# Keys' transposes in another bank, two held steps and a first copy that frees others, in a two-layer hybrid decoder trunk

## The chip, the cores and the metric

The kernel runs on one core of a Trainium2 chip. The metric is device microseconds from start to end of one execution, as the median of several. A core has five engines that run their own instruction rows and wait for each other by semaphores: TensorE (PE; its weight loads are listed as PEld), VectorE (DVE), ScalarE (ACT), GpSimd (POOL) and SyncE (SP), which here only issues transfers. Operands lie in on-chip memory; TensorE writes its results into eight banks of an accumulation memory of 128 x 512 numbers each, from where VectorE and ScalarE read them.

## What is computed

Two layers of a decoder over 256 tokens of width 1024, in 32-bit floats. The core of the reference:

```
for l in range(DEPTH):
    xn = rms_norm(h, norm_mix[l])
    proj = xn @ w_in[l]
    (hq, hf, hi, hg, nq, kc, vc, ksl, vsl, ksw, vsw, ngate) = jnp.split(proj, IN_SPLIT_POINTS, axis=-1)
    o_hg = hgrn2_mixer(hq, hf, hi, hg, lb[l], hg_gnorm[l])
    o_nsa = nsa_mixer(nq, kc, vc, ksl, vsl, ksw, vsw, ngate, ...)
    mix = jnp.concatenate([o_hg, o_nsa], axis=-1)
    h = h + mix @ w_out[l]
    xn = rms_norm(h, norm_ffn[l])
    gu = xn @ w_ffn_in[l]
    h = h + (jax.nn.silu(gu[..., :D_FF]) * gu[..., D_FF:]) @ w_ffn_out[l]
```

The hgrn2 mixer is a gated linear recurrence of 4 heads of 128 (q, forget gate f, input i, output gate g); the nsa mixer has 8 query heads of 64 in two groups and three branches (compressed, selected and sliding-window attention), each with a softmax, weighted by gates. With 256 tokens the selected and the window branch both see all causal keys.

## The kernel before

**Products in three parts.** Each weight matrix comes in units of 128 x 1024 numbers (`unit`, `load_to`). A unit is split into a high part, a rounded copy by ScalarE (`whi`, line 144), and a low part, a subtraction by VectorE (`wlo`, line 145); activations are split the same way. `mm3` (line 330) issues three matmuls per product: high by high, high by low, low by high. All of them are appended to the list `products`, and other steps are tied to a place in it: `after(a, [products[n]])` puts instruction a behind the n-th product in the scheduler's graph, without a wait of its own. Raw loads lie in 4 buffers, split units in 6; `weights(i)` splits up to 5 units ahead of the one in use, so a split may start once the unit six places earlier has been read for the last time.

**The order.** The code names priorities and ties, and a scheduler puts each engine's instructions in one fixed row. Each engine runs its row in that order.

**One layer.** `norm_T` normalises x, turns it on TensorE (`pxn`, line 357), and splits it (`x2`; high part line 362 on ScalarE, low part line 363 on VectorE). The projections follow in the order B (compressed keys and values, selected keys), C (window keys and values, gates), A (queries), first gates, second gates, hi, hg, the output projection `py`, and the feed-forward part (`pgu`, `pz`). In the second layer the first pxn transposes are tied behind product `end + HOLD[0]`, which lies in the last sums of the layer before (`pz`), and the products of C stand partly among those of B.

**Attention, beside the products.** `phid` and `phT`, `pkc` are the compression network; `pkT` its turned key; `pkk` (line 580) the turned selected and window keys, copied to `kA` (ScalarE, line 586) and `kB` (VectorE, line 587); `pqT` the turned queries, copied to `qA`. `scores(t, g)` makes the scores `pS` (for t = 0 a mask matmul first, line 638), the negated maximum `nm`, and the exponentials (`exps`, line 608, ScalarE) with their sums; line 664 and 666 scale them by `cf` on VectorE and ScalarE. `compressed()` is the small branch (`pcs`, `scT`, `pcr`, `pc`, `pcT`). `outputs(t)` turns the probabilities (`pPT`, line 678), copies them to `PT` (ScalarE for g = 0, VectorE for g = 1, line 682) and sums `pO` (line 690).

**Recurrence, beside the products.** From the gates (`FH`, `KH`, `QH`) `pd` and seven levels `pl` (line 806) build the matrix `AT`; VectorE multiplies the decays between levels, and ScalarE copies the levels 6 and 7 into `AT` (line 834). `vh` is the copy of the hi projection (line 759, ScalarE), `sgt` that of hg.

**Banks.** Eight banks under four tags: "a" 2, "b" 2, "c" 3, "e" 1. A tile of a tag waits until the tile that used its bank before has been read. hi and hg use "a" (a bank for each of the two halves of the tokens, so hg's first half takes the bank of hi's first half); pkT, pkk, pqT, pS, pPT, pcs, pcr, pcT use "c"; C, pd, pl use "b".

Of the kernel before, what the change touches and what calls it, by code (L numbers as in the profile page):

```python
# [14 lines left out]
AF = mybir.ActivationFunctionType  # L15
# [3 lines left out]
D, T, NT, NL = 1024, 256, 2, 2  # L19
# [21 lines left out]
AHEAD = 5  # L41
SPLIT_PRIO = 400
LEV_PRIO, BLOCK_PRIO, PACE = 250, 3000, (6, 14)
HOLD, HOLD_C, HOLD_T = (18, 18, 16, 36), 1, 28


def shape_constants():
# [43 lines left out]
def trunk(ctx: ExitStack, tc: tile.TileContext, x, w_in, w_out, lbl, gnorm, q_gain, k_gain,  # L91
          pe_k, w1_k, w2_k, pe_v, w1_v, w2_v, w_ffi, w_ffo, norm_mix, norm_ffn, consts, out):
    nc = tc.nc
    V, S, PE, DMA = nc.vector, nc.scalar, nc.tensor, nc.sync
# [10 lines left out]
    def bank(name, tag):  # L105
        return ps.tile([128, 512], F32, name=name, tag=tag, bufs=BANKS[tag])
# [2 lines left out]
    units = []  # L109

    def unit(src, a, b):
        units.append([src, a, b, None, None, None, None])
        return len(units) - 1

    state = {"loaded": 0, "split": 0}
# [12 lines left out]
    def after(ins, others):  # L128
        for o in others:
            tc.add_manual_dep(ins.ins, o.ins.name,  # L130
                              mybir.DependencyInfo(mybir.DependencyClass.NoSync, mybir.DependencyReason.DATA),
                              reason="fewer table loads")

    def split_to(n):
        while state["split"] < min(n, len(units)):
            load_to(state["split"] + 1)
            u = units[state["split"]]
            a, b = u[1], u[2]
            hi = wsp.tile([128, 1024], F32R, name="whi")
            lo = wsp.tile([128, 1024], F32R, name="wlo")  # L140
            u[4] = hi[:, : a * b].rearrange("p (a b) -> p a b", b=b)
            u[5] = lo[:, : a * b].rearrange("p (a b) -> p a b", b=b)
            with tc.high_priority(offset=SPLIT_PRIO):
                after(S.activation(u[4], u[3], AF.Copy), hi_behind.pop(0) if hi_behind else ())  # L144
                u[6] = V.tensor_sub(u[5], u[3], u[4].bitcast(F32))  # L145
                if lo_behind:
                    after(u[6], lo_behind.pop(0))
                    lo_held.append(u[6])
            state["split"] += 1
# [222 lines left out]
    for l in range(NL):  # L372
# [39 lines left out]
        def proj_tok(name, n=512, tag="a"):  # L412

            for t in range(NT):
                p = bank("pt", tag)
                ts = slice(128 * t, 128 * t + 128)
                for q in range(4):
                    w = weights(U[name, q]) if t == 0 else units[U[name, q]][4:6]
                    for k in range(2):
                        kk = 2 * q + k  # L420
                        mm3(p[:, :n], (X[0][:, kk, ts], X[1][:, kk, ts]), (w[0][:, k], w[1][:, k]),
                            kk == 0, kk == KC - 1)
                yield t, p
# [24 lines left out]
        for t, p in proj_tok("B"):  # L448
            if l and t == 0:
                norm_T(1, gain0, *X[:2], "c", hold=begin + HOLD[1])  # L450
            S.activation(kvc[:, t], p[:, 0:256].rearrange("p (a d) -> p a d", d=64)[:, :, None, :]
                         .to_broadcast([128, 4, 2, 64]), AF.Copy)
            square_k(p[:, 256:384], 0, t)
            S.activation(vtok[:, 0, t], p[:, 384:512], AF.Copy)
            rope_k(p[:, 256:384].rearrange("p (g d) -> p g d", d=64), 0, t)
# [24 lines left out]

        gate = wk.tile([128, NT, 24], F32, name="gate")
        for t, p in proj_tok("C", 280, "b"):
            S.activation(gate[:, t], p[:, 256:280], AF.Sigmoid)
            square_k(p[:, 0:128], 1, t)
            S.activation(vtok[:, 1, t], p[:, 128:256], AF.Copy)
            rope_k(p[:, 0:128].rearrange("p (g d) -> p g d", d=64), 1, t)
# [87 lines left out]

        k8 = kraw.rearrange("p t b (g d) -> p (t b g) d", d=64)
        V.tensor_mul(k8, k8, rs[:, 16:24, None].to_broadcast([128, 8, 64]))
        p = bank("pkk", "c").rearrange("p (b t s) -> p b t s", b=2, t=NT)
        for b in range(2):
            for t in range(NT):
                PE.transpose(p[:, b, t], kraw[:, t, b], ident)  # L580
# [36 lines left out]
        for t in range(NT):  # L617
            nm[t] = sm.tile([128, 2, 4, 2], F32, name="nm")
            rsum[t] = sm.tile([128, 2, 4, 2], F32, name="rsum")
            cf[t] = sm.tile([128, 2, 4, 2], F32, name="cf")  # L620

        def exps(t, p, g, hg):
            for b in range(2):
                exp(P[t, g][:, hg, b], p[:, b], bias=nm[t][:, g, hg, b:b + 1],
                    accum_out=rsum[t][:, g, hg, b:b + 1])

        def scores(t, g):
            if t == 0:
                if g == 0:
                    P0 = wk.tile([128, 2, 4, 2, 128], F32, name="P0", tag="big", bufs=3)  # L630
                    for gg in range(2):
                        P[0, gg] = P0[:, gg]
            else:
                P[1, g] = wk.tile([128, 4, 2, 256], F32, name="P1", tag="big", bufs=3)
            if t == 0:
                for hh in range(2):
                    p = bank("pS", "c").rearrange("p (h b s) -> p h b s", h=2, b=2)
                    PE.matmul(p.rearrange("p h b s -> p (h b) s"), idb, idb4, start=True, stop=False,
                              skip_group_check=True)
                    for i in range(2):  # L640
                        PE.matmul(p[:, i], qA[t][:, g, 2 * hh + i], kA[:, g, :, 0:128], start=False,
                                  stop=False, skip_group_check=True)
                        PE.matmul(p[:, i], qA[t][:, g, 2 * hh + i], kB[:, g, :, 0:128], start=False,
                                  stop=(i == 1), skip_group_check=True)
                    V.tensor_reduce(nm[t][:, g, 2 * hh:2 * hh + 2].rearrange("p h b -> p (h b)"),
                                    p.rearrange("p h b s -> p (h b) s"), axis=AX.X, op=OP.max, negate=True)
                    for i in range(2):
                        exps(t, p[:, i], g, 2 * hh + i)
            else:
                for hg in range(4):  # L650
                    p = bank("pS", "c").rearrange("p (b s) -> p b s", b=2)
                    PE.matmul(p, qA[t][:, g, hg], kA[:, g], start=True, stop=False, skip_group_check=True)
                    PE.matmul(p, qA[t][:, g, hg], kB[:, g], start=False, stop=False, skip_group_check=True)
                    PE.matmul(p[:, :, 128:256], idb, idb4[:, 0:2], start=False, stop=True, skip_group_check=True)
                    V.tensor_reduce(nm[t][:, g, hg], p, axis=AX.X, op=OP.max, negate=True)  # L655
                    exps(t, p, g, hg)
            c = cf[t][:, g].rearrange("p h b -> p b h")
            V.reciprocal(cf[t][:, g], rsum[t][:, g])
            V.tensor_mul(c, c, gv[:, t, 1:3, :, g])
            for hg in range(4):  # L660
                for b in range(2):
                    x, sc = P[t, g][:, hg, b], cf[t][:, g, hg, b:b + 1]
                    if b == 0:
                        V.tensor_scalar(x, x, sc, None, op0=OP.mult)
                    else:
                        S.activation(x, x, AF.Copy, scale=sc)

        def outputs(t):
            po = bank("pO", "e")
            steps = [(b, sb) for b in range(2) for sb in range(t + 1)]  # L670

            def turned(b, sb):

                pts = []
                for g in range(2):
                    p = bank("pPT", "c")
                    for hg in range(4):
                        last = PE.transpose(p[:, 128 * hg:128 * hg + 128],  # L678
                                            P[t, g][:, hg, b, 128 * sb:128 * sb + 128], ident)
                    pt = turn[:, len(turns) % 4]  # L680
                    turns.append(pt)
                    pts.append((pt, V.tensor_copy(pt, p) if g else S.activation(pt, p, AF.Copy)))
                turned.last = [last]
                return pts

# [72 lines left out]
        for t, p in proj_tok("hi"):  # L758
            S.activation(vh[:, t], p, AF.Copy)  # L759
        after(kT, [products[begin + 7]])  # L760
        sgt = wk.tile([128, NT, 512], F32, name="sgt", tag="vs", bufs=2)
        for t, p in proj_tok("hg"):
            V.tensor_copy(sgt[:, t], p)
# [2 lines left out]
        with tc.high_priority(offset=LEV_PRIO):  # L766
# [18 lines left out]
            for lev in range(1, 8):  # L785
# [45 lines left out]
                for n in range(64 // half):  # L831
                    for i in range(2):
                        r0, s0 = 64 * n + half * i, 2 * half * n
                        S.activation(AT[s0:s0 + half, :, i::2, s0 + half:s0 + 2 * half],
                                     pl[r0:r0 + half, :4 * half].rearrange("p (t h a) -> p t h a", t=NT, a=half), AF.Copy)
            p = bank("p8", "b").rearrange("p (h s) -> p h s", s=128)
            for hd in range(4):
                PE.matmul(p[:, hd], KH[:, hd, 0:128], QH[:, hd, 128:256], start=True, stop=True)
# [217 lines left out]
```

## Time and profile before

| | |
|---|---|
| median of 3 runs | 675.47 us (675.41 to 675.97) |
| profiled execution, its own time | 677.52 us |
| its span, first to last instruction | 675.7 us |
| TensorE busy | 658.1 us, 97% of the span |
| VectorE busy | 458.4 us, 68% |
| ScalarE busy | 380.0 us, 56% |
| GpSimd busy | 30.8 us, 5% |
| granted TensorE clock | 1.000 of full speed |

The profile gives for each engine its instructions with their starts and durations, and for an idle stretch the instruction that ended it. Consecutive instructions of one kind are one row, with their count; the ends of matmuls are modelled and neighbours overlap, so the distance from one start to the next is what a step takes of TensorE's time. A row of several matmuls that is longer than their pitch has a wait inside. Idle time on ScalarE or VectorE costs nothing by itself; what they delay on TensorE does.

### The profile page before, as it was taken

To read this page: it belongs to the slowest core of one execution; us is meant where nothing else is said; L and a number is where in the kernel's file an instruction comes from. 1 tells how busy PE (TensorE), PEld (TensorE's weight loads), DVE (VectorE), ACT (ScalarE), POOL (GpSimd) and SP (SyncE) were. 2 spreads that over 40 slices of the span, in tenths; PEclk is the share of its full clock that TensorE was granted. 3 is DMA by queue.
4 is the path that set the end of the run, shared out by engine and by line. 5 is a ranking of instruction groups with operands and counts; after the bars stand their busy time and mean duration, and the time that the engine had idled before them with its cause. 6 is when DMAs were issued, how large, how long until landed. Compare 5 with 4: busy or idle time off the path is not lost.

```text
span 675.7 us, 11741 instructions
## 1 busy us (share of the span) xinstructions
PE 658.1 (97%) x4607; PEld 551.3 (82%) x4607; DVE 458.4 (68%) x767; ACT 380.0 (56%) x670; POOL 30.8 (5%) x67
## 2 busy tenths in 40 slices
PE   5999999999999999999999999999999999999997
PEld 3879876689888888888878897766898888888886
DVE  4878799767665555555578958987676555555552
ACT  5536786836555555555456558685555555555540
POOL 2700001001000000000010000000000000000000
PEclk9999999999999999999999999999999999999999
DMA  7898633254666656656678742432466666666631
GB/s 243 249 346 260 183 72 119 63 184 131 216 186 189 190 191 195 194 193 192 179 239 289 232 125 65 128 95 63 124 215 191 187 186 187 188 190 188 188 120 63
DMA packets 86575, 118.90 MB, mean 176 GB/s; under 512 B 5036, under 2 KB 69366, under 8 KB 86519
## 3 DMA queue, kind: packets, MB, share of 16 engines
q1 hardware_dynamic: 86518, 118.15, 56.9%
q8 instruction: 36, 0.59, 0.4%
q14 instruction: 21, 0.16, 0.1%
HBM read 117.08 MB, written 1.05 MB: 175 GB/s over the span
## 4 chain that ended last, share of the span: by engine, by line
PE 84%; ACT 5%; DVE 4%; DMA 3%; POOL 3%; issue 2%; SPq 0%; DVEq 0%; ACTq 0%; POOLq 0%
PE pgu L940 21%; PE pz L330 17%; PE pgu L944 11%; PE pt L330 10%; PE py L330 6%; PE pq L330 3%; PE pf L330 3%; PE pO L690 2%; DMA wraw<-in_w_in_dram 2%; PE pgt L330 2%; PE pPT L678 1%; ACT whi L144 1%; DVE wlo L145 1%; PE pl L806 1%; ACT P L608 1%
## 5 line engine op out<-in xcount | busy, mean ns | idle before, releaser
L144 ACT ACTIVATE whi<-wraw 128x1024 fp32r<-128x1024 f32 (+1 forms) x204 | 212.7, 1044 | 176.1 <-PE pgu L940 59.1
L145 DVE TENSOR_TENSOR wlo<-wraw,whi 128x1024 fp32r<-128x1024 f32 (+1 forms) x204 | 242.1, 1206 | 59.3 <-ACT whi L144 58.5
L940 PE MATMUL pgu<-x,whi 128*128 128x512 f32 x640 | 152.7, 390 | 0.0
L940 PEld LDWEIGHTS pgu<-x,whi 128*128 128x128 f32 x640 | 118.6, 188 | 23.6
L330 PE MATMUL pz<-whi,ahl 128*128 128x512 f32 x352 | 112.3, 391 | 0.0
L330 PE MATMUL pt<-whi,x 128*128 128x512 f32 (+1 forms) x320 | 97.0, 381 | 0.0
L944 PEld LDWEIGHTS pgu<-x,wlo 128*128 128x128 f32 x640 | 82.1, 191 | 3.1
L944 PE MATMUL pgu<-x,wlo 128*128 128x256 f32 x640 | 83.0, 283 | 0.0
L330 PEld LDWEIGHTS pz<-whi,ahl 128*128 128x128 f32 x352 | 66.0, 188 | 13.9 <-DVE ahl L958 0.5
L330 PE MATMUL pz<-wlo,ahl 128*128 128x512 f32 x176 | 68.8, 391 | 0.0
L330 PEld LDWEIGHTS pt<-whi,x 128*128 128x128 f32 x320 | 57.4, 190 | 9.8 <-ACT vh L759 0.9
L330 PE MATMUL pt<-wlo,x 128*128 128x512 f32 (+1 forms) x160 | 61.2, 382 | 0.7 <-DVE wlo L145 0.7
L955 DVE TENSOR_TENSOR su<-su,pgu 128x256 f32<-128x256 f32 x40 | 16.7, 418 | 50.5 <-ACT su L954 50.5
L949 DVE TENSOR_TENSOR sl<-sl,pgu 128x256 f32<-128x256 f32 x40 | 16.7, 417 | 50.5 <-ACT sl L948 50.5
L330 PE MATMUL py<-whi,x 128*128 128x512 f32 x128 | 42.5, 400 | 0.0
L330 PEld LDWEIGHTS pz<-wlo,ahl 128*128 128x128 f32 x176 | 33.1, 188 | 6.0
L330 PEld LDWEIGHTS pt<-wlo,x 128*128 128x128 f32 x160 | 30.4, 190 | 5.6 <-DVE wlo L145 1.1
L608 ACT ACTIVATE P<-pS,nm 128x128 f32<-128x128 f32 (+1 forms) x64 | 26.2, 429 | 7.1 <-DVE nm L655 6.2
L330 PEld LDWEIGHTS py<-whi,x 128*128 128x128 f32 x128 | 24.1, 188 | 5.3 <-DVE x L707 0.4
L330 PE MATMUL py<-wlo,x 128*128 128x512 f32 x64 | 25.1, 393 | 0.0
L330 PE MATMUL pf<-x,whi 128*128 128x256 f32 x128 | 24.1, 286 | 0.2 <-ACT whi L144 0.2
L330 PE MATMUL pgt<-whi,x 128*128 128x256 f32 x128 | 23.6, 284 | 0.0
(218 smaller groups left out, 808.8 us busy)
## 6 DMA issues: line engine op xcount, KB each, us to landing
wraw<-in_w_ffn_in_dram SPq DMA_DIRECT2D x88, 512.0 KB, 4.5
wraw<-in_w_in_dram SPq DMA_DIRECT2D x48, 512.0 KB, 5.2
wraw<-in_w_ffn_out_dram SPq DMA_DIRECT2D x44, 512.0 KB, 4.0
w<-in_cmp_w_k_dram SPq DMA_DIRECT2D x8, 512.0 KB, 5.0
w<-in_cmp_w_v_dram SPq DMA_DIRECT2D x8, 512.0 KB, 7.0
wraw<-in_w_out_dram SPq DMA_DIRECT2D x16, 256.0 KB, 4.2
wraw<-in_w_out_dram SPq DMA_DIRECT2D x8, 512.0 KB, 4.7
wraw<-in_w_in_dram SPq DMA_DIRECT2D x8, 280.0 KB, 5.6
```

Of the source, the lines that this page charges most:

```text
L144: after(S.activation(u[4], u[3], AF.Copy), hi_behind.pop(0) if hi_behind else ())
L145: u[6] = V.tensor_sub(u[5], u[3], u[4].bitcast(F32))
L330: products.append(PE.matmul(o, a[u], b[v], start=start and i == 0, stop=stop and i == 2, skip_group_check=skip))
L608: e = S.activation(o, i, f, **kw)
L678: last = PE.transpose(p[:, 128 * hg:128 * hg + 128], P[t, g][:, hg, b, 128 * sb:128 * sb + 128], ident)
L690: m = PE.matmul(po[64 * g:64 * g + 64], vtok[:, b, sb, 64 * g:64 * g + 64], pts[g][0], start=(b == 0 and sb == 0), stop=False, skip_group_ ...
L806: m = PE.matmul(o, a, b, start=True, stop=True)
L940: products.append(PE.matmul(pp[b], w[hh][0][:, k, s], X[2][:, 4 * hh + k].rearrange("p c t -> p (c t)"), start=(hh == 0 and k == 0), stop= ...
L944: products.append(PE.matmul(pp[b][:, T:], w[hh][1][:, k, s], X[0][:, 4 * hh + k], start=False, stop=(hh == 1 and k == 3), skip_group_check ...
L949: V.tensor_add(sl[:, b], sl[:, b], pp[b][:, :T])
L955: V.tensor_add(su[:, b], su[:, b], pp[b][:, :T])
```

## The change

Five edits:

- `pkk` takes a bank of tag "b" instead of "c", and is therefore no longer in a row with pkT and pqT for their banks.
- `HOLD_S = 12`: the first mask matmul of the scores is tied behind the 13th product of hi.
- `HOLD[0]` goes from 18 to 21: the second layer's first pxn transposes are tied three products later.
- In the second layer the high part of the second unit of A is tied behind the copy `kvc` of the second half of the tokens (`kept`); entry 7 of a unit now keeps its high part's instruction.
- The copies of levels 6 and 7 into `AT` are tied behind the first copy `PT` of `outputs(0)` (`freed`).

```diff
-HOLD, HOLD_C, HOLD_T = (18, 18, 16, 36), 1, 28
+HOLD, HOLD_C, HOLD_T, HOLD_S = (21, 18, 16, 36), 1, 28, 12
...
-                after(S.activation(u[4], u[3], AF.Copy), hi_behind.pop(0) if hi_behind else ())
+                u[7] = S.activation(u[4], u[3], AF.Copy)
+                after(u[7], hi_behind.pop(0) if hi_behind else ())
...
-            S.activation(kvc[:, t], p[:, 0:256].rearrange("p (a d) -> p a d", d=64)[:, :, None, :]
+            kept = S.activation(kvc[:, t], p[:, 0:256].rearrange("p (a d) -> p a d", d=64)[:, :, None, :]
...
         for t, p in proj_tok("C", 280, "b"):
+            if l and t == 0:
+                after(units[U["A", 1]][7], [kept])
...
-        p = bank("pkk", "c").rearrange("p (b t s) -> p b t s", b=2, t=NT)
+        p = bank("pkk", "b").rearrange("p (b t s) -> p b t s", b=2, t=NT)
...
-                    PE.matmul(p.rearrange("p h b s -> p (h b) s"), idb, idb4, start=True, stop=False,
-                              skip_group_check=True)
+                    masks.append(PE.matmul(p.rearrange("p h b s -> p (h b) s"), idb, idb4, start=True, stop=False,
+                                           skip_group_check=True))
...
                     pts.append((pt, V.tensor_copy(pt, p) if g else S.activation(pt, p, AF.Copy)))
+                    if not freed:
+                        freed.append(pts[0][1])
...
         after(kT, [products[begin + 7]])
+        after(masks[0], [products[begin + HOLD_S]])
...
-                        S.activation(AT[s0:s0 + half, :, i::2, s0 + half:s0 + 2 * half],
-                                     pl[r0:r0 + half, :4 * half].rearrange("p (t h a) -> p t h a", t=NT, a=half), AF.Copy)
+                        m = S.activation(AT[s0:s0 + half, :, i::2, s0 + half:s0 + 2 * half],
+                                         pl[r0:r0 + half, :4 * half].rearrange("p (t h a) -> p t h a", t=NT, a=half), AF.Copy)
+                        after(m, freed)
```

No instruction is added or taken away; the rows of the engines change their order, and the numbers of lines behind the changes rise by 1 to 11.

**ScalarE, first layer, from the last exponentials of the first half of the queries to the copies of hi.** pt_1228 and pt_1282 are the two halves of hi, whi_1310 and whi_1322 the first and the second unit of the output projection that is split here, pc the compressed branch's scores. Before:

```order
L608 ACTIVATE P0_947,rsum_942<-pS_991,nm_941 128x128 x2
L719 ACTIVATE scT_1029<-pcs_1012 128x256
L144 ACTIVATE whi_1310<-wraw_1233 128x1024
L759 ACTIVATE vh_1227<-pt_1228 128x512
L144 ACTIVATE whi_1322<-wraw_1246 128x1024
L759 ACTIVATE vh_1227<-pt_1282 128x512
L666 ACTIVATE P0_947<-P0_947,cf_943 128x128 x4
L608 ACTIVATE pc_1034<-pc_1034 128x256
```

After:

```order
L144 ACTIVATE whi_1310<-wraw_1233 128x1024
L671 ACTIVATE P0_947<-P0_947,cf_943 128x128 x2
L144 ACTIVATE whi_1322<-wraw_1246 128x1024
L671 ACTIVATE P0_947<-P0_947,cf_943 128x128
L611 ACTIVATE pc_1034<-pc_1034 128x256
L768 ACTIVATE vh_1227<-pt_1228 128x512
L768 ACTIVATE vh_1227<-pt_1282 128x512
```

Both vh copies moved from around whi_1322 to behind it, behind a scaling and behind the exponential of pc.

**TensorE, first layer, at the keys' transposes and the first scores.** pf_811 are the second gates' first products, pd the recurrence's first block. Before:

```order
L567 MATMUL pkT_770<-cst_81,kcb_760 128x32
L580 MATMUL pkk_777<-cst_81,kraw_223 128x128 x4
L594 MATMUL pqT_790<-cst_81,qn_467 128x128 x4
L594 MATMUL pqT_801<-cst_81,qn_467 128x128 x4
L775 MATMUL pd_1386<-Q_221,K_220 32x32 x32
```

After, in two pieces, the keys' transposes and then the queries' and the first scores:

```order
L532 MATMUL phT_737<-cst_81,hid_735 128x64 x2
L583 MATMUL pkk_777<-cst_81,kraw_223 128x128 x4
L331 MATMUL pf_811<-x2_130,whi_575 128x256 x2
...
L570 MATMUL pkT_770<-cst_81,kcb_760 128x32
L597 MATMUL pqT_790<-cst_81,qn_467 128x128 x4
L597 MATMUL pqT_801<-cst_81,qn_467 128x128 x4
L331 MATMUL pt_1228<-whi_842,x2_130 128x512 x2
L785 MATMUL pd_1386<-Q_221,K_220 32x32 x32
```

pkk moved from behind pkT, in the products of hi, to ahead of the second gates.

**VectorE at the start of the second layer.** wlo_3492 and wlo_3504 are the low parts of the third and the fourth unit of B, h the residual, x2_3545 the low part of the turned x. Before:

```order
L145 TENSOR_TENSOR wlo_3492<-wraw_3419,whi_3491 128x1024
L363 TENSOR_TENSOR x2_3545<-pxn_3554,x2_3545 128x4x128
L1022 TENSOR_TENSOR h_76<-pz_2072,h_76 128x512
L363 TENSOR_TENSOR x2_3545<-pxn_3561,x2_3545 128x4x128
L145 TENSOR_TENSOR wlo_3504<-wraw_3425,whi_3503 128x1024
```

After:

```order
L146 TENSOR_TENSOR wlo_3492<-wraw_3419,whi_3491 128x1024
L146 TENSOR_TENSOR wlo_3504<-wraw_3425,whi_3503 128x1024
L1033 TENSOR_TENSOR h_76<-pz_2072,h_76 128x512
L364 TENSOR_TENSOR x2_3545<-pxn_3554,x2_3545 128x4x128
L364 TENSOR_TENSOR x2_3545<-pxn_3561,x2_3545 128x4x128
```

The fourth unit's low part and the addition to h moved ahead of both low parts of x; on ScalarE, in the same way, whi_3503 moved ahead of both high parts of x.

## Rows read from the trace of the kernel before

**Rows 1.** The page's part 1: busy us (share of the span) and instructions, TensorE.

```profile
PE   658.1 (97%) x4607; PEld 551.3 (82%) x4607; DVE 458.4 (68%) x767; ACT 380.0 (56%) x670; POOL 30.8 (5%) x67
```

**Rows 2.** TensorE's waits: instruction, releaser, us in total, times, longest.

```profile
PE pS L638 <- DVE kB L587: 1.0, 2, 0.5
...
PE pkc L541 <- DVE hk L537: 0.8, 1, 0.8
```

**Rows 3.** TensorE's timeline at the first scores: start, us, instruction, count, idle before.

```profile
82.22 0.62 PE L330 MATMUL pt<-whi,x 128*128 128x512 f32 x2
82.67 0.39 PE L330 MATMUL pt<-wlo,x 128*128 128x512 f32 x1
83.57 0.39 PE L638 MATMUL pS<-cab,idb 128*128 128x512 bf16 x1 [0.51 <-DVE kB L587]
```

**Rows 4.** ScalarE's timeline around the copies of hi, first layer.

```profile
96.75 0.58 ACT L759 ACTIVATE vh<-pt 128x512 f32<-128x512 f32 x1
97.39 1.06 ACT L144 ACTIVATE whi<-wraw 128x1024 fp32r<-128x1024 f32 x1
98.36 0.58 ACT L759 ACTIVATE vh<-pt 128x512 f32<-128x512 f32 x1
98.84 1.27 ACT L666 ACTIVATE P<-P,cf 128x128 f32<-128x128 f32 x4
100.86 0.42 ACT L608 ACTIVATE pc<-pc 128x256 f32<-128x256 f32 x1 [0.75 <-DVE pc L732]
```

**Rows 5.** TensorE's timeline from hi to hg, first and second layer.

```profile
96.96 0.91 PE L330 MATMUL pt<-whi,x 128*128 128x512 f32 x2
...
425.47 0.91 PE L330 MATMUL pt<-whi,x 128*128 128x512 f32 x2
```

**Rows 6.** TensorE's timeline in the outputs, first layer.

```profile
112.51 0.66 PE L678 MATMUL pPT<-cst,P 128*128 128x128 f32 x4 [0.31 <-ACT PT L682]
113.10 1.40 PE L690 MATMUL pO<-PT,vtok 128*64 128x512 f32 x4
114.43 0.50 PE L652 MATMUL pS<-kA,qA 128*128 128x512 f32 x1
...
116.75 1.08 PE L690 MATMUL pO<-PT,vtok 128*64 128x512 f32 x4
117.76 1.16 PE L702 MATMUL pO<-pcT_sb,vblk 128*128 128x128 f32 x8
...
127.11 1.61 PE L678 MATMUL pPT<-cst,P 128*128 128x128 f32 x12
...
133.25 1.94 PE L690 MATMUL pO<-PT,vtok 128*64 128x512 f32 x8
```

**Rows 7.** TensorE's timeline at the second layer's start.

```profile
343.75 0.63 PE L357 MATMUL pxn<-cst,xn 128*128 128x128 f32 x4 [0.51 <-DVE xn L345]
...
346.28 0.62 PE L330 MATMUL pt<-whi,x 128*128 128x512 f32 x2
```

**Rows 8.** ScalarE's and VectorE's timelines there.

```profile
343.85 0.18 ACT L339 ACTIVATION_READ_ACCUMULATOR xn<-h 128x1 f32 x1
...
346.33 0.68 ACT L144 ACTIVATE whi<-wraw 128x560 fp32r<-128x560 f32 x1
...
344.18 1.22 DVE L145 TENSOR_TENSOR wlo<-wraw,whi 128x1024 fp32r<-128x1024 f32 x1
...
346.01 0.69 DVE L1022 TENSOR_TENSOR h<-pz,h 128x512 f32<-128x512 f32 x1
```

**Rows 9.** TensorE's timeline at the compression's transposes, second layer.

```profile
359.88 0.87 PE L465 MATMUL pa<-cst,kvc 128*128 128x128 f32 x6 [0.30 <-ACT kvc L451]
```

**Rows 10.** TensorE's timeline at the kernel's start.

```profile
11.12 1.97 PE L357 MATMUL pxn<-cst,xn 128*128 128x128 f32 x8 [4.90 <-DVE xn L345]
...
13.94 1.05 PE L330 MATMUL pt<-whi,x 128*128 128x512 f32 x2
14.79 0.45 PE L330 MATMUL pt<-wlo,x 128*128 128x512 f32 x1
```

More of the change, by code (lines that the diff above doesn't have):

```diff
@@ L111, in unit @@
     def unit(src, a, b):
-        units.append([src, a, b, None, None, None, None])
+        units.append([src, a, b] + [None] * 5)
         return len(units) - 1
@@ L620, in trunk @@
             cf[t] = sm.tile([128, 2, 4, 2], F32, name="cf")
+        masks = []
         def exps(t, p, g, hg):
@@ L666, in scores @@
                         S.activation(x, x, AF.Copy, scale=sc)
+        freed = []
         def outputs(t):
```

## Prediction

> **What bounds the kernel now.** I read the busy shares first, then what TensorE waits for, then the timeline of the places the diff touches. TensorE is busy 658.1 us of a span of 675.7 [rows 1], so the end moves only by what is added to or taken from TensorE's own row: a wait, or an interruption of its row of products. The profiled execution took 677.52 us against a median of 675.47; differences are summed on the former and set on the latter. The list of waits names few in the two attention stages: the scores for kB 1.0 us in two layers, pkc 0.8 [rows 2]. It names no wait where a row of two products simply took longer, and one such row matters below.
>
> **Keys' transposes earlier, first mask held.** In the first layer the last group of products before the first scores starts at 82.67, its scores at 83.57: 0.90 us where a product takes 0.23 (two in the 0.45 from 82.22), of which 0.51 is idle on kB [rows 3]; the 0.16 that is left is what an interruption of the row costs. The wait of pS comes twice, once a layer [rows 2]. In the changed order pkk and its copies run during the second gates, and products stand between pqT and the scores, so kB is long there. I take 0.6 a layer as gained, between 0 (the scores then wait for qA, which is copied in the same few us) and 0.67. The pkc wait (0.8, on hk) stays: pkk's four transposes stand ahead of it, but nothing that makes hk is earlier; a gain of at most 0.5 is left to the range.
>
> **ScalarE around vh: the term that decides.** TensorE's first product of hg writes the bank that hi's first token left, so it waits for the first vh copy. Before, that copy stands ahead of the split of the second of wo's weights (whi_1322): vh starts 96.75, the split 97.39, the second vh 98.36 [rows 4]. After, ScalarE's row is: split, one scaling of P, the exponential of pc, and only then vh. That split writes the memory of the last weights of hi (six buffers in a ring), so it may not start before the 48th, last product of hi has read them; and the 49th may not start before vh. TensorE therefore stands still for the whole chain, whatever else goes well. Before, the row of two from 96.96 took 0.91 us and one product takes 0.39 [rows 3], so the 49th began at 97.48 [rows 5]: 0.52 after the 48th, 0.29 more than the pitch of 0.23. After, from the start of the 48th: 0.43 until the split starts (97.39 less 96.96), 0.97 the split (98.36 less 97.39), 0.32 a scaling (1.27 for four), 0.33 the exponential (0.42 less the 0.09 by which neighbours overlap), 0.58 vh, and 0.15 until TensorE starts (97.48 less 96.75 and 0.58) [rows 4, 5]. The sum is 2.78, a stop of 2.55, so **+2.26 us** a layer. The second layer has the same row of two at 425.47, 0.91 [rows 5], and the changed order is the same there. Bounds: +1.9 if the split is let go 0.1 sooner and the neighbours overlap more, +2.6 if the exponential comes late. The row shows ScalarE taking instructions strictly one behind another. The Trainium skill's page PSUM — Partial Sum Buffer, section Engine vs sequencer instructions, says that too, "ScalarE/VectorE/GpSimdE queues are strict FIFO"; if ScalarE could take vh past the waiting split, this term would be nothing and the sum 675.1, but row and page both speak against that.
>
> **Level 6 and 7 copies held behind the first PT copy.** This turns the whole tail of the attention: the pPT of outputs(0) stand in one row, outputs(1) comes earlier, the levels later. Counts are the same. Before, waits lie in four kinds of places: pPT for PT (112.51, 0.31 idle), pO after it (113.10 to 114.43 is 1.33, where the same four take 1.01 from 116.75 to 117.76) [rows 6], and likewise two rows of pO and pPT of outputs(1); I read them together as an estimate at 1.8 us, from 0.43 and 0.24 around 112.51, 0.32 behind it, and 0.83 in seven rows between the twelve transposes at 127.11 and the eight pO at 133.25, the first and the last of them [rows 6] (1.53 for the twelve where eight take 0.85, and so on). After, pO of outputs(0) waits for VectorE's copy of PT, which stands behind the level's decay (about 1.0), and that of outputs(1) behind the next level's (about 0.85): about the same 1.85. Two interruptions fewer at 0.16 are -0.32, and the last transposes wait a little more (+0.1). I take **-0.15** a layer, between -2.0 (all waits gone) and +0.6. A layer then gives 2.26 - 0.6 - 0.15 = **+1.5**, two layers +3.0. SyncE's issue of w1's fourth part now stands ahead of the last wo load and two ffn_in loads. It waits for the last reader of PT, which is earlier in the new order, and what it passes is used later than that, so I cost it nothing; without that cover a load of 4 to 5 us would stop TensorE for a part of itself.
>
> **The layer boundary.** HOLD[0] puts three products more before the next layer's first pxn. The wait there was 0.51 [rows 7], three products are 0.68, so it goes. But the order on ScalarE and VectorE changes as well: the split of the last B weights stands ahead of both copies of x's high part, and VectorE does that split's low part and the residual's addition ahead of x's low part. ScalarE: the square ends at 344.03 (343.85 and 0.18), the split takes until 345.0, two copies at 0.5 (vh's size [rows 4], less the overlap) until 346.0, then a split of 560 columns (0.68, less the overlap) until 346.6 [rows 8]. VectorE: wlo until 345.31, the next wlo until 346.45 (1.22 each, less the overlap), the addition until 347.05 (0.69), x's low part, as wide, until 347.7 [rows 8]. TensorE's third B product needs x's low part: it began at 346.28 [rows 7] and would begin at about 347.7, +1.4. A product of C that is now pulled in there is worth 0.1, and the kvc copy put ahead of a split takes some 0.2 from pa's wait of 0.30 [rows 9]. **+1.1**, from -0.8 (only the two waits go) to +1.6.
>
> **Sum.** +3.0 + 1.1 = +4.1 on 677.52, that is 681.6 as profiled and **679.6** as a median.
>
> **Rivals.** Faster: the tail heals itself. TensorE comes 1.7 us later to the tail in each layer, while ScalarE and VectorE stay on time, so their copies lie ready: all 1.8 of waits go and the new ones don't come, a layer gives 2.26 - 0.6 - 2.1 = -0.45, and with the boundary's -0.8 the median is 673.8. It decides from the point where pO and pPT of outputs(0) find PT ready; for it speaks that before only some tenths are missing at each place [rows 6], against it that vh's delay is a delay of ScalarE too, since the exponentials of the second half stand behind it. No change: the tail heals as above, but the boundary costs its 1.1: 2 x -0.45 + 1.1 is +0.2, 675.7; or half of either, up to 676.8. The clock: TensorE stood still for 4.90 us before 11.12, and the products that followed took 0.43 each (two in the 0.85 from 13.94 to 14.79) against 0.23 [rows 10]: the lower of its two levels, 1.2 GHz against 2.4, though the profile's clock column shows 1.00. If the stop of 2.55 us does the same, five products cost about 1.0 more, 2.0 in two layers: 681.6. [...]
>
> **How the numbers follow.** Forecast 679.6: 0.68 (its own range 677.3 to 681.2). The clock: 0.08. No change: 0.16. Faster: 0.08. Runs of this kernel tell about 0.2%, 1.35 us, from no change: faster 0.08, same 0.16, slower 0.68 + 0.08 = 0.76. The range of 8 in 10 leaves out the faster case and most of the lower half of no change: 675.9 to 682.0.
>
> **What would show it.** In the changed trace: a gap of about 2.5 us on TensorE before the first hg product of each layer, with vh as releaser and a split just before it on ScalarE; no wait of pS on kB; pxn of the second layer without a wait, but a wait of a microsecond on x (from VectorE) at the third product of B; pO waits on PT of about 1 us in each outputs. If the gap before hg is under 1.5 us, the main step is wrong; if the gap is there and the time is unchanged, the tail's slack is what I sized wrongly; if products behind the gap take 0.43, it is the clock.

## The result: slower by 1%, a little more than the range allowed

The changed kernel takes **683.64 us** (four runs, 681.09 to 685.02) against 675.72 us, a ratio of 1.0105 (95% interval 1.0087 to 1.0123). Forecast were 679.6 us and a range up to 682.0: the direction was right, the size was not, by 4 us. The profiled execution took 683.9 us with a span of 682.1 and a mean granted clock of 0.995.

**TensorE's waits after** (instruction, releaser, us in total, times, longest), the view of [rows 2]:

```profile
PE pt L331 <- ACT vh L768: 4.8, 2, 2.4
PE pxn L358 <- DVE xn L346: 4.8, 2, 4.5
...
PE pt L331 <- DVE x L364: 0.8, 1, 0.8
```

The wait of pS on kB of [rows 2] is gone. In its place stands a wait for vh, the copy of the hi projection, 2.4 us in each layer.

**TensorE's timeline at that place, first and second layer** (start, us, instruction, count, idle before and its releaser), which answers [rows 5]:

```profile
96.01 0.39 PE L331 MATMUL pt<-whi,x 128*128 128x512 f32 x1
98.78 0.50 PE L331 MATMUL pt<-whi,x 128*128 128x512 f32 x1 [2.38 <-ACT vh L768]
...
99.36 0.63 PE L331 MATMUL pt<-whi,x 128*128 128x512 f32 x2
...
100.10 1.05 PE L331 MATMUL pt<-whi,x 128*128 128x512 f32 x2
101.09 1.06 PE L816 MATMUL pl<-Q,K 128*32 128x16 f32 x64
...
430.69 0.50 PE L331 MATMUL pt<-whi,x 128*128 128x512 f32 x1 [2.39 <-ACT vh L768]
```

The 49th product starts 2.77 us after the 48th; the prediction's chain gave 2.78. A little later two products take 1.05 where two took 0.63, and the 64 small matmuls of a level 1.06 where they take 0.73 to 0.74 elsewhere. In the second layer the two products from 431.37 to 432.23 are 0.43 each, which the prediction had named as the sign of the clock.

**ScalarE's timeline there**, which answers [rows 4]:

```profile
95.06 1.06 ACT L144 ACTIVATE whi<-wraw 128x1024 fp32r<-128x1024 f32 x1
96.03 0.68 ACT L671 ACTIVATE P<-P,cf 128x128 f32<-128x128 f32 x2
96.61 1.04 ACT L144 ACTIVATE whi<-wraw 128x1024 fp32r<-128x1024 f32 x1
97.56 0.39 ACT L671 ACTIVATE P<-P,cf 128x128 f32<-128x128 f32 x1
97.85 0.40 ACT L611 ACTIVATE pc<-pc 128x256 f32<-128x256 f32 x1
98.16 1.05 ACT L768 ACTIVATE vh<-pt 128x512 f32<-128x512 f32 x2
```

ScalarE has no idle time of 0.15 us or more in these rows. The split at 96.61 comes straight out of two scalings, 0.60 after the 48th product had started, and the scaling, the exponential and vh follow it in the same way. So here it is ScalarE's own full row that makes vh late, and not a wait of that split for the product at 96.01, which the prediction had as the first link.

**The clock in short stretches** (stretch, its length, TensorE's busy us and instructions, granted clock, then share and rate of transfers):

```profile
98.80:100.00 1.20, 1.20 (x5) 1.00 1.15 219
100.00:101.00 1.00, 1.00 (x3) 0.51 0.80 250
101.00:102.00 1.00, 1.00 (x65) 0.50 0.99 393
102.00:103.00 1.00, 1.00 (x14) 0.50 0.83 336
103.00:104.00 1.00, 1.00 (x7) 0.79 0.09 29
...
431.00:433.00 2.00, 2.00 (x6) 0.53 1.02 262
433.00:435.00 2.00, 2.00 (x68) 0.62 0.88 342
```

The same stretches before:

```profile
100.00:102.00 2.00, 2.00 (x18) 1.00 1.01 250
...
430.00:432.00 2.00, 2.00 (x71) 1.00 0.98 393
```

TensorE had stood still, started again at 98.78, and from 100.0 ran some 3 us at the lower of its levels, 1.2 GHz instead of 2.4; in the second layer the same shows from 431.1, 0.4 us after it had started again. Before, the clock is 1.00 there.

**The second layer's start**, TensorE's timeline, which answers [rows 7], and VectorE's, which answers [rows 8]:

```profile
346.10 0.62 PE L358 MATMUL pxn<-cst,xn 128*128 128x128 f32 x4
...
350.14 0.73 PE L331 MATMUL pt<-whi,x 128*128 128x512 f32 x2 [0.83 <-DVE x L364]
```

```profile
346.53 2.35 DVE L146 TENSOR_TENSOR wlo<-wraw,whi 128x1024 fp32r<-128x1024 f32 x2
348.80 0.68 DVE L1033 TENSOR_TENSOR h<-pz,h 128x512 f32<-128x512 f32 x1
349.40 1.28 DVE L364 TENSOR_TENSOR x<-pxn,x 128x512 fp32r<-128x512 f32 x2
```

pxn no longer waits, and the third B product waits for x's low part, which stands behind two split parts and the addition. The last pgu product had started 2.37 later than before; 350.14 less 2.37 is 347.77, where the prediction said 347.7.

**Where the time went, by stretches.** Differences to the profiled execution of before, from the starts of the same instructions in the traces: the compression's phT, hi's last product (48th), hg's first (49th), the last poT transpose, and, for the boundary, from the last pgu to the second layer's phT.

| stretch, us | before | change | pkk alone | vh first | stop filled | vh before pc | shorter stop |
|---|---|---|---|---|---|---|---|
| layer 1, phT to 48th | 34.44 | -0.38 | -0.14 | +0.37 | -0.12 | -0.57 | -0.67 |
| layer 1, 48th to 49th | 0.42 | +2.36 | +2.35 | +0.30 | +2.36 | -0.01 | +1.40 |
| layer 1, 49th to poT | 49.64 | +1.48 | +1.51 | -0.04 | +0.50 | -0.17 | +1.03 |
| layer 2, phT to 48th | 33.89 | -0.92 | -0.90 | -0.90 | -0.93 | -0.90 | -0.90 |
| layer 2, 48th to 49th | 0.41 | +2.36 | +2.36 | +0.31 | +2.37 | +0.00 | +1.41 |
| layer 2, 49th to poT | 49.69 | +1.45 | +1.39 | -0.02 | +0.51 | -0.10 | +1.05 |
| boundary | 58.61 | +1.00 | -0.12 | +1.01 | +1.02 | -0.45 | +1.01 |

The kernels of the other columns follow now. The first row scatters by up to a microsecond among kernels whose TensorE work there is alike, and is -0.19 in a second profiled execution of the change; pf on wlo and pkc on hk wait between 0.3 and 1.2 us in all of them. The rows around the stop repeat to about a tenth in kernels with the same order. The boundary does not always: the second execution of the change shows +2.62 there, as told below.

### The profile page after: what moved, and what is told of

Its sections match the earlier page's. It is cut to its first block, busy times and chain, and to the rows that moved or that the text cites. A ratio compares the mean times of both kernels' runs of the same rounds, so it can differ in the third digit from the quotient of the medians.

```text
span 682.1 us, 11745 instructions
## 1 busy us (share of the span) xinstructions
PE 662.6 (97%) x4607; PEld 553.4 (81%) x4607; DVE 458.8 (67%) x767; ACT 381.6 (56%) x670; POOL 27.0 (4%) x67
## 3 DMA queue, kind: packets, MB, share of 16 engines
HBM read 117.08 MB, written 1.05 MB: 173 GB/s over the span
## 4 chain that ended last, share of the span: by engine, by line
PE 88%; DVE 4%; DMA 3%; ACT 3%; issue 1%; POOL 0%; SPq 0%; DVEq 0%; ACTq 0%; POOLq 0%
PE pgu L951 21%; PE pz L331 17%; PE pt L331 12%; PE pgu L955 11%; PE py L331 6%; PE pgt L331 3%; DMA wraw<-in_w_in_dram 3%; PE pq L331 3%; PE pf L331 2%; PE pO L699 2%; PE pPT L685 2%; PE pl L816 1%; ACT whi L144 1%; DVE wlo L146 1%; PE pxn L358 1%
## 5 line engine op out<-in xcount | busy, mean ns | idle before, releaser
L331 PE MATMUL pt<-whi,x 128*128 128x512 f32 (+1 forms) x320 | 98.5, 386 | 6.2 <-ACT vh L768 4.8
```

The lines of the kernel that those rows point to most:

```text
L331: products.append(PE.matmul(o, a[u], b[v], start=start and i == 0, stop=stop and i == 2, skip_group_check=skip))
```

## Experiments

### One edit carries the loss

Does the stop come from the bank of pkk, or from the ties? Two kernels: the change with this one line put back, and before with this one line alone.

```diff
-        p = bank("pkk", "b").rearrange("p (b t s) -> p b t s", b=2, t=NT)
+        p = bank("pkk", "c").rearrange("p (b t s) -> p b t s", b=2, t=NT)
```

> The change with pkk put back into a bank of tag c; all other edits stay. TensorE's and ScalarE's rows in the attention are then those of before but for one pair of transposes. Theory (the bank's tag alone turns the rows around vh, and with them come the stop of 2.5 us before hg and the low clock behind it, about 5 us of the 7 or 8): no stop and no low clock in either layer, the wait of pS on kB is back, the boundary's +1.0 stays, so about 676.7 (676.0 to 677.5). Rival (the copies held behind PT, or the boundary, make the loss): 680 or more.

Measured: 677.06 us, before 675.56, ratio 1.0020 (1.0011 to 1.0030). TensorE's waits:

```profile
PE pS L643 <- DVE kB L590: 1.0, 2, 0.5
PE pt L331 <- DVE x L364: 0.8, 1, 0.8
```

No wait for vh, the clock 1.000 in the profiled run, and of the losses the boundary's +1.02 alone is left. (Two of the ten runs, 677.52 and 677.65, show a mean clock of 0.997.)

> The kernel before with the one edit that pkk takes a bank of tag b. Theory: the same stop before hg in both layers, 2.4 us on vh, and the low clock behind it (0.5 for about 3 us, 1.6 us lost each), boundary as before: 681.5 (680 to 683). Rival (it takes the other edits for the stop, or the early scores pay for it): within 1.5 of before, 674.5 to 677.

Measured: 683.42 us, a little over the stated range, ratio 1.0113 (1.0091 to 1.0135). TensorE's waits, and the clock in two stretches behind the first layer's stop:

```profile
PE pt L330 <- ACT vh L759: 4.8, 2, 2.4
```

```profile
99.00:101.00 2.00, 1.69 (x5) 0.68 0.95 225
101.00:103.00 2.00, 2.00 (x60) 0.50 0.99 379
```

The tag of one tile is the whole loss of the attention, and the tie of levels 6 and 7 has no part in it: this kernel lacks the tie, and in the attention its ScalarE and VectorE rows are those of the change, while TensorE's differ only around the first mask matmul. Through the bank the scheduler places pkk and its copies otherwise, and everything behind it on ScalarE turns with it.

### The stop taken away

```diff
+        after(units[U["wo", 4]][7], vhs[:1])
```

(vhs holds the two vh copies; the split of the first output unit, and by the order of the ring the second, stand behind the first of them.)

> The change with one more tie: the split of the first of the output projection's units (and with it the second) stands behind the first vh copy on ScalarE. Theory: no stop before hg, no low clock, the earlier first scores stay a gain of 0.6 a layer, the boundary's +1.0 stays: about 675.5 (674.5 to 677). Rival (ScalarE's row is full there, so what vh no longer waits for, the exponentials and splits behind it do): the stop comes back in smaller pieces at pS, pPT or the wlo of wo, 678.5 or more.

Measured: 677.40 us, ratio 1.0030 (1.0013 to 1.0047), 6.2 less than the change, 1.9 more than expected and just over the stated range. Two of its five runs show a mean clock of 0.997 and 0.996 (678.00 and 679.16). Of its waits, TensorE still has one for vh, 0.7 in two layers, since vh now stands behind the exponential of pc:

```profile
PE pt L331 <- ACT vh L769: 0.7, 2, 0.3
```

Behind the 49th product it takes as long as before (-0.04 and -0.02): what the stop costs after itself is gone with it.

### The stop kept, the clock held

```diff
+            if t == 1:
+                fill = [products[begin + 47]]
+                for i in range(NFILL):
+                    m = PE.matmul(p, none, units[U["hg", 0]][4][:, i % 2], start=False, stop=False, skip_group_check=True)
+                    after(m, fill)
+                    fill = [m]
...
+        after(products[begin + 48], fill)
```

NFILL is 9 and `none` a tile of zeros; the result stays what it was.

> The change with nine more products of 512 columns between the last product of hi and the first of hg in each layer; their stationary operand is zero and they add to hi's second bank, so nothing else changes. They fill 2.0 us of the stop of 2.5 and end before vh does, so the stop costs the same and only the clock can change. Theory (the stop is what lowers the clock, and the low clock is 1.6 us a layer): clock 1.000 throughout, products behind the stop at 0.23, time 3.2 less than the change's, about 680.4 (679.7 to 681.2), and little spread between runs. Rival (the slow products behind the stop come from something else, as the loads that start then): 0.43 a product as before, 683 to 684.

Measured: 682.25 us, ratio 1.0100 (1.0079 to 1.0121). TensorE's timeline and the clock:

```profile
95.98 0.40 PE L334 MATMUL pt<-whi,x 128*128 128x512 f32 x1
96.22 2.26 PE L774 MATMUL pt<-whi,none 128*128 128x512 f32 x9
98.76 0.50 PE L334 MATMUL pt<-whi,x 128*128 128x512 f32 x1 [0.29 <-ACT vh L777]
...
100.03 0.63 PE L334 MATMUL pt<-whi,x 128*128 128x512 f32 x2
```

```profile
100.00:102.00 2.00, 2.00 (x72) 1.00 1.01 326
102.00:104.00 2.00, 2.00 (x12) 1.00 0.46 178
```

From 95.98 to 98.76 is 2.78, the stop of the change to 0.01; the difference is that TensorE works in it. The clock stays at 1.00 and two products take 0.63 again. So the idle stop lowers the clock, not the loads that run at the time (their shares are alike). The size was not as expected, and the time, 682.25, lies over the stated range: from the 49th product to poT the kernel gains 0.98 and 0.94 a layer, not 1.6. More of the gain is there earlier. The first transposes of the outputs, in the change and in this kernel:

```profile
108.01 2.00 PE L685 MATMUL pPT<-cst,P 128*128 128x128 f32 x16
```

```profile
106.56 2.00 PE L688 MATMUL pPT<-cst,P 128*128 128x128 f32 x16
```

From the 49th product to there it is 9.23 in the change and 7.80 here, 1.4 less, and the same in the second layer; up to there the rows of TensorE are the same. Behind it they are not, though the expectation took nothing else to change: with the nine products the scheduler placed the tail otherwise. Four products of the scores stand between the two halves of the first outputs' sums, and VectorE's copies and maxima have other places. So the low clock costs 1.4 a layer up to the outputs. Whether the 0.45 that is gone by poT is slack in the tail, or the other order, is not shown.

The runs of both kernels lie far apart; the next two experiments take both side by side, with more runs.

> The changed kernel as it is, once more and oftener, beside the next one on the same chip, to size what the clock costs and what spread it brings. Theory: 683.5 (682.5 to 684.5), runs between 681 and 685, the slower the lower their mean clock (0.999 to 0.994). Rival (the clock's share was chance of four runs): 682 or less, within half a microsecond of the kernel with the stop filled.

Measured: 683.51 us, ratio 1.0114 (1.0091 to 1.0136), runs from 680.36 to 685.96, wider than expected. The profiled execution is the slowest of them, 685.96 with a mean clock of 0.993. Its rows are those of the first profiled one, and so are its stretches to 0.2, but for the boundary, +2.62 instead of +1.00. TensorE's timeline there, and the clock:

```profile
350.54 0.82 PE L331 MATMUL pt<-whi,x 128*128 128x512 f32 x2 [0.82 <-DVE x L364]
```

```profile
351.00:353.00 2.00, 2.00 (x7) 0.51 1.09 369
```

This wait is the last of three, 0.24, 0.31 and 0.82, in the first products of the second layer. The first execution has the same three (0.24, 0.31 and 0.83) and a clock of 1.00 behind them. So the clock can fall at the boundary as well, in one execution and not in another, and costs 1.6 there; not all of the spread between runs comes from the stop before hg. Where it fell in the runs that were not profiled is not known.

> The kernel with the stop filled by nine products into hi's second bank (its stationary operand zero), once more and oftener. In the profiled runs it is 1.0 faster in each layer from the first hg product to the last poT than the change. Theory: 1.4 to 2.2 under the change of this call, about 681.7, at clocks of 0.997 to 1.000. Rival: no difference to the change beyond its interval.

Measured: 682.42 us, ratio 1.0104 (1.0088 to 1.0121); 1.1 less than the change, under the forecast 1.4 to 2.2, and the intervals overlap, so the medians alone do not separate the two kernels. The change's own ten runs fall apart: 680.36, 681.09 and 681.75 us at a mean clock of 0.999, and seven from 683.22 to 685.96 (middle 683.9) at 0.997 to 0.991. The same program is some 2.8 us slower where the mean clock is lower, in which at least one run counts a fall at the boundary. Eight of the ten runs of the filled kernel show 0.999 or 1.000, two show 0.997 (683.41 and 685.42); both of its profiled runs have 1.00 behind the stops. Their median of 682.4 lies 1.3 us over the middle one of the change's three quick runs; what the nine products themselves cost was not measured apart. Over the runs the clock's share is between 1.1 and 2.8 us.

### A shorter stop

```diff
+        after(units[U["wo", 5]][7], vhs[:1])
```

(Only the second output unit's split goes behind vh, which still stands behind the first one, three scalings and the exponential.)

> The change with only the second output unit's split behind the first vh copy: vh still stands behind three scalings and the exponential of pc, behind the first unit's split. From the rows of the change: split until 96.0, 0.97 for the scalings, 0.33, 0.58 and 0.15: the first product of hg 2.0 after the last of hi, a stop of 1.8 instead of 2.5. Theory (the stop costs its length and 0.2 of lateness in the tail, in each layer; whether the clock falls depends on the stop): without a fall 2 x (2.0 less 0.7) more than with vh first, 680.0, with the fall of the change (1.0 a layer) 682. Rival (the cost is all or nothing, as some other engine sets the time of the tail): 683, like the change, or 677.5, like vh first.

Measured: 681.28 us (679.85, 681.17, 681.38 and 686.03), ratio 1.0096 (1.0058 to 1.0134). TensorE's timeline at the stop, and the clock there and behind it:

```profile
94.62 0.39 PE L331 MATMUL pt<-whi,x 128*128 128x512 f32 x1
96.44 0.50 PE L331 MATMUL pt<-whi,x 128*128 128x512 f32 x1 [1.43 <-ACT vh L769]
```

```profile
96.00:98.00 2.00, 1.56 (x6) 1.00 0.91 242
98.00:99.00 1.00, 1.00 (x66) 1.00 0.98 205
```

The stop goes with the length of the row ahead of vh, neither all nor nothing, and the clock stays at 1.00 in the profiled run; three runs show a mean of 0.999, one 0.994, and that one is the 686.03. Behind the 49th product it loses 1.03 without any fall of the clock, more than the filled kernel with its longer stop (0.50). The rows of ScalarE and VectorE in the tail differ between the two, so what lateness alone costs the tail of the change is not settled by either.

### The boundary

On the kernel with vh first: HOLD[0] back at 18, and, apart from that, 21 with the splits behind x.

```diff
-HOLD, HOLD_C, HOLD_T, HOLD_S = (21, 18, 16, 36), 1, 28, 12
+HOLD, HOLD_C, HOLD_T, HOLD_S = (18, 18, 16, 36), 1, 28, 12
```

> The kernel with vh first (the change, and the split of the first output unit behind the first vh copy, 677.4), with HOLD[0] back at 18. The rows of ScalarE, VectorE and TensorE at the second layer's start are then those of before. Theory (the +1.0 at the boundary comes from the order that 21 brings there, the split and its low part ahead of x): from the end of pgu to phT of the second layer the 1.0 goes, 676.4 (675.7 to 677.1), and pxn waits its 0.5 again. Rival (the tie of A's second unit to kvc, which stays, makes the loss): 677.4, the 1.0 stays.

Measured: 675.45 us, ratio 1.0004 (0.9991 to 1.0017), 2.0 under vh first and just under the stated range; the boundary is at -0.33 instead of +1.01, and pxn waits 0.50 again. The other 0.6 between the medians, which come from different calls, was not located. The tie to kvc stays in this kernel; pa's wait of [rows 9] is not among its waits.

```diff
+        if l:
+            after(units[U["B", 3]][7], last)
+            after(units[U["B", 3]][6], low)
```

(last is the second high part of x, low its two low parts; on VectorE the split's low part now stands behind them.)

> The kernel with vh first, HOLD[0] at 21, and one more tie: the high part of B's fourth unit stands behind the high parts of x, its low part behind the low parts of x. The third product of B then doesn't wait for a split. Theory (only the order behind the three more products costs, the hold itself covers the wait of pxn): no wait of pxn, no wait of a microsecond on x, so the 1.0 goes and 0.3 to 0.5 more: 675.9 (675.2 to 676.6). Rival (the products end three earlier than x is ready however the rows stand, since pxn itself is later): the wait moves to the copies of x, 676.9 to 677.5.

Measured: 675.78 us, ratio 0.9996 (0.9987 to 1.0006), boundary -0.45. No wait of pxn there, 0.3 on x:

```profile
342.54 0.62 PE L358 MATMUL pxn<-cst,xn 128*128 128x128 f32 x4
...
344.84 0.73 PE L331 MATMUL pt<-whi,x 128*128 128x512 f32 x2 [0.27 <-DVE x L364]
```

The three more products were no mistake by themselves: with the splits ahead of x the boundary is at +1.01, with the splits behind it at -0.45, and at -0.33 without them. The order they brought was the loss; by themselves they win 0.1 in the trace and nothing that the medians of the two kernels show.

### Toward a better kernel

The last one with the exponential of pc behind the first vh copy, too:

```diff
+        after(pce[0], vhs[:1])
```

> As the one with x first, and the first vh copy also stands ahead of the exponential of pc. Where vh is first but for that exponential, TensorE still waits 0.3 in each layer before hg. Theory: these two waits go, the tail of the attention stays as it was: 0.6 less than with x first alone, 675.3 (674.6 to 676.0). Rival (pc is then late by the two splits, and pcT and the sums that need it pay): the 0.6 comes back as a wait of pcT or pO, 675.9 to 677.

Measured: 674.57 us, ratio 0.9984 (0.9971 to 0.9997), just under the stated range. ScalarE's timeline around vh, and one row of TensorE's:

```profile
94.97 0.57 ACT L774 ACTIVATE vh<-pt 128x512 f32<-128x512 f32 x1
95.44 1.99 ACT L144 ACTIVATE whi<-wraw 128x1024 fp32r<-128x1024 f32 x2
97.34 0.40 ACT L615 ACTIVATE pc<-pc 128x256 f32<-128x256 f32 x1
```

```profile
95.18 0.91 PE L331 MATMUL pt<-whi,x 128*128 128x512 f32 x2
```

The row of two products takes 0.91 again, as in [rows 5], and the late exponential costs nothing (-0.17 and -0.10 behind it).

> The kernel with vh ahead of the exponential of pc and x first, once more and oftener. Theory: 674.4 (673.8 to 675.0), 1.2 under before, its interval clear of none. Rival (the 0.16% of three rounds was chance): 675 to 676.

Measured: 674.69 us (eleven runs), ratio 0.9988 (0.9980 to 0.9997): a little faster than before, by about 1 us, and clear of no change.

> The same without the hold of the first mask matmul; only TensorE's row changes, the first scores stand four products earlier behind the queries' transposes. Theory (the queries' copies are then what the scores wait for, and the products that would cover it stand behind): a wait of pS on qA of 0.5 to 0.9 in each layer, of which the earlier scores give back little: 675.4 (674.6 to 676.4), 1.0 over the kernel above. Rival (the scores find their operands ready): no wait, the exponentials 0.5 earlier, 674.0 to 674.6.

Measured: 675.01 us, ratio 0.9991 (0.9980 to 1.0001), the same as with the hold. The expectation was wrong: the waits name none of pS on qA or kB, and the first scores' operands are ready at once after the recurrence's first block. The hold of the first mask is worth nothing that was measured.

## Why the prediction was right in direction and short in size

**ScalarE around vh, +2.26 a layer: right in size, with its first link wrong.** Measured +2.36 in both layers: split, scaling, exponential, vh, one behind another. The 0.10 between is a reading of before: the 49th product began at 97.38, 0.42 after the 48th and not 0.52, since the second of those two takes 0.50, as the 49th does after. That 2.77 met the chain's 2.78 is in part luck: until the split starts it is 0.60 instead of 0.43, as ScalarE is still busy with two scalings, and from vh's end to TensorE's start 0.05 instead of 0.15. That ScalarE works through its row in order, as the Trainium skill's page PSUM — Partial Sum Buffer, section Engine vs sequencer instructions, says as well, the trace after agrees with: the last product of hi's first half starts at 86.65, and its copy vh at 98.16, when its turn comes.

**The clock: put at nothing in the sum, and this is the step that failed.** The prediction had it as a rival, at a chance of 0.08 and 2.0 us. It came, at 0.50 to 0.53 for some 3 us behind each stop. Nothing in the rows spoke against it: products took 0.43 behind the one long stop that before has [rows 10]. With a stop of 2.5 us as the central forecast, its consequence belonged into the sum, or at least into the range. It does not come every time: three of the change's ten runs show 0.999. The Trainium skill's page TensorE: Matmul & The Clock Gate, section Why this matters for your kernels, warns of idle gaps between bursts of matmuls. The windows after agree that such a gap lowers the clock, but not on its length: this one, 2.4 us idle, is shorter than those that the page warns of. The price in the profiled runs: 1.4 a layer up to the outputs, 1.0 by the end of the attention in a kernel whose rows differ by then (1.48 less 0.50); 1.1 to 2.8 us over the runs. The three runs of the change at 0.999 lie between 680.4 and 681.8, within the range.

**The tail, -0.15: mis-sized, and for the wrong reason.** Of the +1.48, 1.4 is the low clock's up to the outputs; with the clock held it was +0.50 (stop filled), and without the stop -0.04 and -0.02 (vh first), both with other rows in the tail. So the tail of the change itself lost between some 0.1 and 0.5. The tie of levels 6 and 7, to which the prediction gave the new order, is not what makes it: pkk alone brings the same rows without the tie. The rows of the outputs after show the waits that were forecast, with other sizes:

```profile
109.94 2.42 PE L699 MATMUL pO<-PT,vtok 128*64 128x512 f32 x8
...
122.19 1.81 PE L699 MATMUL pO<-PT,vtok 128*64 128x512 f32 x4
```

The eight of outputs(0) last 2.35 to the next start where twice four took 2.02 [rows 6], 0.33 instead of 1.0; the four of outputs(1) 1.75 instead of 1.01, 0.74 for the forecast 0.85. The rest lies in other small places, and its cause was not taken apart.

**Earlier scores, -0.6: right in kind.** The wait on kB is gone. Up to the 48th product the second layer gains 0.92, in which a wait of 0.42 among the small matmuls that only the old order has (the kernel with pkk in c has it too) goes as well: about 0.5 is left. The first layer gains 0.38, of which 0.27 is pkc's shorter wait on hk; with the scatter of that row, its share is not resolved.

**The boundary, +1.1: right.** Measured +1.00, with pxn's wait gone and 0.83 on x as written. In the second profiled execution a fall of the clock, which no term had, adds 1.6.

**The sum.** By layers 3.46 and 2.89, and 1.00 at the boundary are 7.35; forecast were 4.1. Of the 3.25 between, the clock and the tail are 3.2 together, 1.9 to 2.8 of it the clock's, the stop 0.2 and the earlier scores in the first layer 0.2, less 0.3 of gain in the second and 0.1 at the boundary. The spans of the two profiled executions differ by 6.4 only (682.1 less 675.7): outside these stretches the change's is 1.0 quicker, 0.57 ahead of the first layer's phT and 0.52 in its feed-forward part, where all the traces scatter. The medians differ by 7.9, since the profiled execution of before was a slow one (677.52 against 675.72). So of the 4.0 by which the median was missed 2.3 lie in the profiled times (683.9 against 681.6), and 1.7 in setting a sum over one execution on a median. The rivals on the other side, a tail that heals itself and no change, needed the tail to take back 2 us; it took back nothing.

## What to carry to other kernels

A tile's bank tag is an instruction to the scheduler: moving one transpose turned the rows of an engine 30 us later, so read the new rows of every engine, not the diff. On an engine that runs in order, look for a copy that frees a bank and stands behind a full row of other work; that row is a stop of the engine that needs the bank, and its length can be added up before running, from the last place where both engines' times are known. And where a forecast holds a stop of TensorE of microseconds, give what the clock takes behind it a place in the sum or the range.

## What the hardware showed that was not expected

The clock does not fall at a fixed distance from the stop: in the first profiled execution of the change 1.2 us after TensorE has started again in the first layer and 0.4 us in the second, in the other one, in the first layer, while it still stood, before the product at 98.62:

```profile
98.40:98.60 0.20, 0.00 (x0) 0.63 0.98 225
```

It comes back after some 3 us (0.51, 0.50, 0.50, 0.79). Three short waits in a row, 0.24, 0.31 and 0.82 us, were followed by the lower level in one execution and not in the other. The same program shows a mean of 0.999 in some executions and 0.991 in others, 680.4 to 686.0 us, so a kernel with such a stop is also an unsteady one: before spread over 674.3 to 677.1 in the same call. Products with a stationary operand of zeros held the clock at 1.00 at the stops of both profiled runs that had them.
